# A hybrid decoder block in fp32 on one core: a buffer pool for the gates' results, gate 5 one product later, three buffers for pieces of the weights' sums

## The chip, the cores and the metric

The kernel runs on one core of a Trainium2 chip. A core has a matrix engine (TensorE, PE in the profile; its weight loads are PEld), three engines for elementwise work (VectorE or DVE, ScalarE or ACT, GpSimd or POOL) and a queue (SyncE, SP) that issues its transfers. Each engine works through its own instructions in a fixed order and waits for the others by semaphores. Matrix products land in PSUM, of which the kernel uses eight banks of 128 x 512 numbers; everything else on the chip is in SBUF, 128 partitions wide.

The metric is the time of one execution on the device, in microseconds. A run of the kernel gives one time; three runs were made of the kernel before.

## The reference

One layer of a block over 512 tokens of width 1024, in float32. Cut to what matters:

```python
h = rmsnorm(x, norm1_g)
z_glu, z_rx, z_rg, z_ga, z_gb = split(h @ w_in + b_in)    # 2048, 1280, 1280, 1024, 1024 wide

u = z_glu[..., :1024] * sigmoid(z_glu[..., 1024:])
u = causal_depthwise_conv(u, conv_dw_w, conv_dw_b)         # 31 taps
u = silu(layernorm(u, conv_ln_g, conv_ln_b))
y_a = u @ conv_w_out + conv_b_out

xb = causal_depthwise_conv(z_rx, lru_conv_w, lru_conv_b)   # 4 taps
r = sigmoid(blocks(xb, lru_wa) + lru_ba)                   # 16 blocks of 80 x 80
i = sigmoid(blocks(xb, lru_wx) + lru_bx)
log_a = -8 * r * softplus(-lru_lambda)
hb = scan(h_t = exp(log_a) * h_(t-1) + sqrt(-expm1(2 * log_a)) * i * xb)
y_b = (hb * gelu(z_rg)) @ lru_w_out

x = x + (sigmoid(z_ga) * y_a + sigmoid(z_gb) * y_b) @ w_mix_out
h = rmsnorm(x, norm2_g)
x = x + (silu(h @ ffn_w1) * (h @ ffn_w3)) @ ffn_w2         # 2816 wide
return rmsnorm(x, norm_f_g)
```

## The kernel before

**Products.** Tokens lie along the 512 columns, channels along the 128 partitions. To keep float32's precision every operand is kept as two parts, a high one (`h`, rounded to the fast matrix format) and a low one (`l`, the rest), and a product is three matrix instructions: high x high, high x low, low x high (`mm3`, L432). The high part is a cast on ACT (`split_to`, L115, cast at L117), the low part a subtraction (`sub`, L113) on DVE or POOL. A product of the input stage (1024 channels in, 128 out) is 24 instructions on PE.

**Weights** come in chunks. `emit_chunk` (L135) loads one into one of four raw buffers (SP's queue, L144), casts it on ACT and subtracts on POOL (input stage) or DVE (later), into one of five buffers `hl`. A product asks for its chunk, and so four chunks ahead are emitted with it (`AHEAD`, L35). A gate's chunk is a zeroed buffer into which 6 to 10 small loads (L188) put the blocks of 80 x 80; for even gates (counted within each half of five) a small copy on DVE (L193) follows.

**The input stage** (`ORDER`, L201 to 203, run at L763 to 782) lists its products by hand, and the chunks of weights are listed in the same order (L205 to 212):
- `u` j: two products of the conv branch and u_j (`glu`, L657; L664 on DVE). The 31-tap convolution over u is a generator, `beside` (L588), of which each entry of the list emits a few steps (L600 on DVE, in PSUM); after it come the layer norm's two column means, each a product with a matrix of ones (`column_mean`, L607; PSUM tiles lnmp and lnvp), and `un`, the operand of conv_w_out. The sums' split parts are the tiles lnms and lnvs.
- `rx` j: a product, the 4-tap convolution into `xb`j (L676 on ACT, L678 on DVE), its two parts xb`j`h and xb`j`l, and copies of some of their rows to other partitions (`ext_in`, L689; transfers at L701 into the tiles `ext`), since a block of 80 channels straddles tiles of 128.
- `g` j: the two gates r and i of channels tile j (`gates`, L706): eight or twelve instructions on PE into two banks, L726 to L731 on ACT, L732 to L735 on DVE. Their lasting results are two tiles, `th`j and `ea`j.
- `r` j: the recurrence (`recur`, L740): a square root on ACT into a bank `mu`j (L743), a product on DVE (L744) and the scan (L745).
- `rg`, `gb`, `ga` j: a product each; y_j (two parts) from `rg` (L756 to 760), the sigmoids sgb_j and sga_j from the others (L752).

Then come eight products with lru_w_out (`yb`, L785 to 794), eight with conv_w_out (`ya`, L896 to 904) and the mixing product (`mxr`).

**Sevenfold products.** w_mix_out, four of the feed-forward's tiles (`SEVEN`, L44) and ffn_w2 are multiplied with seven products of quarters in place of eight. That needs sums of the weights' quarters. For the feed-forward, `make_f_sums` (L315) makes them during the input stage: sixteen pieces, each two loads (L334) into a buffer of the pool `wsums`, four operations on POOL (L342 to 345) and a store (L349). One step of it is taken with each entry of `ORDER`. The pool has two buffers. The operands' sums are made in `Sevenfold.pair` (L825): the tiles us (two parts), s1p (two halves), e and va for each k; there are eleven k in the last product (names `ou`, `ov`, `ous`, `os1p`, `oe`). In `run` (L846) the tiles e and va are split in their turn (`oeb`, `ovb`), and with k = 0 the residual (x2b, eight tiles) and norm_f_g (gf, two) are loaded (`loads`, L1073).

**Buffers.** Most tiles of 128 x 512 that outlive a step come from one pool, `longt` (L95), with `SLOTS` = 65 buffers of 2 KB per partition; short-lived ones from `shortt`, with 5. Six PSUM banks belong to the pool `psum` (`bank`), two to `psum2` (`bank2`). The whole of SBUF is in use.

**The order of instructions.** Where the kernel says nothing else, a planner orders each engine's instructions when the kernel is compiled: it goes through a model of the run, takes on every engine the ready instruction that stands first in the program's text, and gives a new tile a buffer when one is free. The buffer, the order and the waits are then fixed. Parts of the kernel (norms, the ends of the sevenfold products) are ordered by hand (`manual_schedule`).

Of the kernel before, what the change touches and what calls it, by code (L numbers as in the profile page):

```python
# [28 lines left out]
NF = DF // P  # L29


SLOTS, SHORT = 65, 5
RAW = 4
HL = 5
AHEAD = 4  # L35
# [45 lines left out]
def tile_block(ctx, tc, a, out):  # L81
    nc = tc.nc
    pool = lambda name, bufs, **k: ctx.enter_context(tc.tile_pool(name=name, bufs=bufs, **k))
    consts = pool("consts", 1)
    raws = pool("raws", RAW)
    hls = pool("hls", HL)
    wsums = pool("wsums", 2)
    psum = pool("psum", 6, space=bass.MemoryType.PSUM)
    psum2 = pool("psum2", 2, space=bass.MemoryType.PSUM)

    def tiles(tag, bufs):
        p_ = pool(tag, bufs)
        return lambda name, dtype=F32: p_.tile([P, T], dtype, tag=tag, name=name)

    longt, shortt = tiles("long", SLOTS), tiles("short", SHORT)  # L95

    def pairt(name, dtype=F32R):

# [2 lines left out]
    def bank(name):  # L101
        return psum.tile([P, T], F32, tag="mm", name=name)
# [9 lines left out]
    def sub(eng, o, x, y):  # L112
        return eng.tensor_tensor(out=o, in0=x, in1=y, op=ALU.subtract)  # L113

    def split_to(h, l, full, eng, copy=act.copy):  # L115

        copy(h, full)  # L117
        last = sub(eng, l, full, h.bitcast(F32))
        if eng is pool_e:
            newest["sub"] = last.ins  # L120
        return h, l

    def split(name, full, eng, p_=None, copy=act.copy):
        p_ = p_ or pairt(name)
        return split_to(*p_, full, eng, copy)
# [35 lines left out]
    def weights(key, ahead=AHEAD):  # L161
        i = next(i for i, c in enumerate(chunks) if c[0] == key)
        emit_to(i + 1 + ahead)
        return held.pop(key)
# [14 lines left out]
    def gate_chunk(j):  # L179
# [18 lines left out]

    ORDER = """u0 u1 rx0 rx1 gb0 rx2 u2 g0 rx3 gb1 g1 u3 rx4 g2 gb2 r0 r1 u4 g3 rx5 rg0 g4 rx6 rg1 u5 r2 r3 g5 rx7  # L201
        gb3 rg2 rx8 g6 rg3 u6 r4 r5 g7 rx9 gb4 rg4 u7 g8 r6 r7 rg5 gb5 g9 rg6 gb6 r8 r9 rg7 gb7 ga0 rg8 ga1 rg9
        ga2 ga3 ga4 ga5 ga6 ga7""".split()
    ORDER = [(t.rstrip("0123456789"), int(t.lstrip("abcdefghijklmnopqrstuvwxyz"))) for t in ORDER]
    for kind, j in ORDER:  # L205
        if kind == "g":
# [336 lines left out]
    ab, e, s, s2, po, c4 = (sm[:, i, :] for i in range(6))  # L543
# [162 lines left out]
    def gates(j):  # L706
        hv, lv = (gate_view(v[:, 0, :]) for v in weights(f"gate{j}"))
        j5 = j % 5
        banks = []
        for g in range(2):  # L710
            ps = bank(f"g{j}_{g}")
            (wh, oh), (wl, ol) = ((v[:, g, 0, :], v[:, g, 1, :]) for v in (hv, lv))
            xh, xl = xbp[j]
            mms = [(wh, xh), (wh, xl), (wl, xh)]
            if j5 % 2:
                eh, el = ext[j]
                mms += [(l[:MANY], r[:MANY]) for l, r in ((oh, eh), (oh, el), (ol, eh))]
            else:
                mms.append((oh[: 3 * FEW], ext[j][0][: 3 * FEW]))
            for k, (l, r) in enumerate(mms):  # L720
                pe.matmul(ps, l, r, start=k == 0, stop=k == len(mms) - 1)  # L721
            banks.append(ps)

        r_, i_ = banks
        th = longt(f"th{j}")
        act.activation(th, r_, AF.Tanh, scale=0.5, bias=bh[:, 0, j : j + 1])  # L726
        act.activation(i_, i_, AF.Tanh, scale=0.5, bias=bh[:, 1, j : j + 1])  # L727

        A = longt(f"ea{j}")
        act.activation(A, th, AF.Exp, scale=c8[:, j : j + 1], bias=c8[:, j : j + 1])  # L730
        act.activation(r_, th, AF.Tanh, scale=c4[:, j : j + 1], bias=c4[:, j : j + 1])  # L731
        vec.scalar_tensor_tensor(out=r_, in0=A, scalar=1.0, in1=r_, op0=ALU.add, op1=ALU.mult)  # L732
        vec.scalar_tensor_tensor(out=xb[j], in0=i_, scalar=1.0, in1=xb[j], op0=ALU.add, op1=ALU.mult)
        vec.tensor_scalar(out=A, in0=r_, scalar1=1.0, scalar2=None, op0=ALU.add)
        vec.scalar_tensor_tensor(out=th, in0=A, scalar=1.0, in1=r_, op0=ALU.add, op1=ALU.mult)  # L735
        rec[j] = A, th

    rec = {}

    def recur(j):  # L740
        A, m2 = rec.pop(j)
        mu = bank(f"mu{j}")
        act.activation(mu, m2, AF.Sqrt, scale=-0.25)  # L743
        vec.tensor_tensor(out=mu, in0=xb[j], in1=mu, op=ALU.mult)  # L744
        vec.tensor_tensor_scan(xb[j], A, mu, 0.0, op0=ALU.mult, op1=ALU.add)  # L745
# [16 lines left out]
    f_sums_steps = make_f_sums()  # L762
    for kind, j in ORDER:  # L763
        next(f_sums_steps, None)
        if kind == "u":
            glu(j)
        elif kind == "rx":
            rx(j)
            run_beside(4)
        elif kind == "g":  # L770
            gates(j)
        elif kind == "r":
            recur(j)
        elif kind == "rg":
            rg(j)
            run_beside(6)
        elif kind == "gb":
            sig(GB, j, sgb, "sgb")
            run_beside(6)
        else:  # L780
            sig(GA, j, sga, "sga")
            run_beside(8)
# [27 lines left out]
    class Sevenfold:  # L810
# [14 lines left out]
        def pair(self, k, ua, va):  # L825

            n = self.name
            u_ = split(f"{n}us{k}", ua, vec)
            s1 = shortt(f"{n}s1{k}")[:, LO]
            add(s1, va[:, LO], va[:, HI])  # L830
            sp = longt(f"{n}s1p{k}", F32R)
            split_to(sp[:, LO], sp[:, HI], s1, vec)
            e = longt(f"{n}e{k}")
            sub(vec, e[:, HI], ua[:, LO], va[:, LO])
            sub(vec, va[:, LO], s1, ua[:, LO])
            sub(vec, e[:, LO], ua[:, HI], va[:, LO])
            self.ops.append((u_, sp, e, va))
# [58 lines left out]
    for n, j in enumerate(mixq.order()):  # L896
# [3 lines left out]
        o = sga[j]  # L900
# [262 lines left out]
```

## Time and profile before

| | us |
|---|---|
| three runs: lowest, median, highest | 814.56, 814.58, 815.5 |
| the profiled execution, on the device | 814.25 |
| its span, from the first to the last instruction | 812.5 |
| PE busy, DVE busy, ACT busy, POOL busy | 799.8, 647.2, 445.2, 210.4 |
| input stage's products on PE | 10 to 325 |
| products with lru_w_out, conv_w_out | 325 to 380, 380 to 423.5 |
| mixing product, feed-forward's first half | 423.5 to 463, 463 to 700.5 |
| product with ffn_w2 and the end | 700.5 to 812.5 |

The granted clock of TensorE was 0.998 of full speed. Times inside the execution are counted from its first instruction. In a list of waits a line reads: engine, tile and line that waited, what ended the wait, then microseconds in total, how often, the longest. In a timeline: start, duration, engine, line, operation, what it writes and reads, and in brackets how long the engine had been idle and what ended that. A chain of waits gives start, duration and what the time was spent in. Buffer numbers are left out of a tile's name where they stand at its end (xb for xb5), and kept inside it (xb7l).

### The profile page before, as it was taken

Reading aid. Unit: us, or ns where it says so; the run is one execution under the profiler, and the core shown is the slowest. Engines: PE = TensorE matmul, PEld = TensorE weight load, DVE = VectorE, ACT = ScalarE, POOL = GpSimd, SP = SyncE. Lnnn points to the kernel's source line nnn. Section 1 sums busy time; section 2 is a strip of 40 time slices with the busy share of each in tenths; the row PEclk is TensorE's granted clock in tenths of the full one; section 3 lists DMA queues with packets and bytes.
Section 4 is the critical chain, followed back from the end, with each engine's and each line's share of the span. In section 5 each row is a group of like instructions: output and inputs, shape, how many; then the busy total and the mean of one; then the engine's idle time right before and its main releaser. Section 6 shows DMA issues by size and latency. Waiting matters only on the chain.

```text
span 812.5 us, 11454 instructions
## 1 busy us (share of the span) xinstructions
PE 799.8 (98%) x4038; PEld 682.0 (84%) x4038; DVE 647.2 (80%) x1010; ACT 445.2 (55%) x627; POOL 210.4 (26%) x156
## 2 busy tenths in 40 slices
PE   8999999999999999999999999999999999999996
PEld 7988888887788888888888898999988888888885
DVE  4699899999999987786968769797866664688556
ACT  7546688777668755653326554464632233476443
POOL 3575778758666740000000042000000000000000
PEclk9999999999999999999999999999999999999999
DMA  7746566666655622358628425788778788576552
GB/s 214 190 128 164 143 176 199 172 189 193 185 169 156 183 74 65 111 177 275 215 93 259 156 88 181 237 266 247 226 235 279 250 274 284 195 255 211 169 168 104
DMA packets 182029, 153.46 MB, mean 189 GB/s; under 512 B 12519, under 2 KB 150163, under 8 KB 181971
## 3 DMA queue, kind: packets, MB, share of 16 engines
q1 hardware_dynamic: 181971, 152.72, 61.2%
q8 instruction: 32, 0.52, 0.3%
q14 instruction: 26, 0.21, 0.1%
HBM read 123.46 MB, written 26.21 MB: 184 GB/s over the span
## 4 chain that ended last, share of the span: by engine, by line
PE 93%; DVE 3%; issue 1%; ACT 1%; DMA 1%; SPq 0%; POOL 0%; POOLq 0%; ACTq 0%
PE z L441 32%; PE f L441 19%; PE or L844 13%; PE fr L1020 10%; PE yb L441 7%; PE ya L441 5%; PE mxr L844 5%; PE g L721 2%; DVE cv L600 1%; DMA raw_in<-in_w_in_dram 1%; PE th L481 0%; DVE xb8l L113 0%; PE tx L481 0%; DVE of L1086 0%; DVE x L497 0%
## 5 line engine op out<-in xcount | busy, mean ns | idle before, releaser
L600 DVE SCALAR_TENSOR_TENSOR cv<-u,par,cv 128x511 f32<-128x511 f32 (+17 forms) x240 | 162.5, 728 | 1.1 <-ACT cv L597 0.9
L113 POOL TENSOR_TENSOR hl_in<-raw_in,hl_in 128x1024 fp32r<-128x1024 f32 x52 | 125.5, 2416 | 91.1 <-ACT hl_in L117 90.5
L117 ACT CAST hl_in<-raw_in 128x1024 fp32r<-128x1024 f32 x52 | 54.2, 1042 | 9.4 <-PE z L441 6.6
L117 ACT CAST hl_f<-raw_f 128x1024 fp32r<-128x1024 f32 x28 | 29.3, 1051 | 49.8 <-DMA raw_f<-in_ffn_w_dram 31.3
L113 DVE TENSOR_TENSOR hl_f<-raw_f,hl_f 128x1024 fp32r<-128x1024 f32 x28 | 36.3, 1304 | 15.9 <-ACT hl_f L117 15.9
L994 POOL TENSOR_TENSOR hf<-h20h,h20l 128x512 f32<-128x512 f32 x1 | 1.3, 1288 | 172.4 <-DVE h20l L485 172.4
L117 ACT CAST hl_ob<-raw_ob 128x1024 fp32r<-128x1024 f32 (+1 forms) x23 | 23.4, 1016 | 39.0 <-PE or L844 18.7
L441 PE MATMUL z<-h10h,hl_in 128*128 128x512 f32 (+1 forms) x112 | 42.3, 379 | 1.7 <-DVE xb L745 1.2
L113 DVE TENSOR_TENSOR hl_ob<-raw_ob,hl_ob 128x1024 fp32r<-128x1024 f32 (+1 forms) x23 | 27.1, 1176 | 20.5 <-ACT hl_ob L117 20.4
L441 PE MATMUL z<-h11h,hl_in 128*128 128x512 f32 (+1 forms) x112 | 41.7, 374 | 0.0
L441 PE MATMUL z<-h15h,hl_in 128*128 128x512 f32 (+1 forms) x112 | 41.7, 374 | 0.0
L441 PE MATMUL z<-h17h,hl_in 128*128 128x512 f32 (+1 forms) x112 | 41.7, 374 | 0.0
L441 PE MATMUL z<-h14h,hl_in 128*128 128x512 f32 (+1 forms) x112 | 41.7, 374 | 0.0
L441 PE MATMUL z<-h16h,hl_in 128*128 128x512 f32 (+1 forms) x112 | 41.7, 374 | 0.0
L441 PE MATMUL z<-h12h,hl_in 128*128 128x512 f32 (+1 forms) x112 | 41.7, 374 | 0.0
L441 PE MATMUL z<-h13h,hl_in 128*128 128x512 f32 (+1 forms) x112 | 41.7, 374 | 0.0
L113 POOL TENSOR_TENSOR fws<-fws 128x256 f32<-128x256 f32 x48 | 36.3, 757 | 2.6 <-DMA fws<-in_ffn_w_dram 0.2
L113 DVE TENSOR_TENSOR ows<-ows,ows 128x512 f32<-128x512 f32 x22 | 15.2, 689 | 20.9 <-DMA ows<-in_ffn_w_dram 20.8
L113 DVE TENSOR_TENSOR hl_ot<-raw_ot,hl_ot 128x1024 fp32r<-128x1024 f32 (+1 forms) x17 | 20.1, 1190 | 11.8 <-ACT hl_ot L117 11.4
L117 ACT CAST hl_ot<-raw_ot 128x1024 fp32r<-128x1024 f32 (+1 forms) x17 | 17.5, 1028 | 17.2 <-PE or L844 13.9
L441 PEld LDWEIGHTS z<-h10h,hl_in 128*128 128x128 f32 x112 | 21.1, 188 | 6.5 <-ACT g L727 1.6
L441 PEld LDWEIGHTS z<-h11h,hl_in 128*128 128x128 f32 x112 | 21.1, 188 | 3.8
(905 smaller groups left out, 2577.4 us busy)
## 6 DMA issues: line engine op xcount, KB each, us to landing
raw_in<-in_w_in_dram SPq DMA_DIRECT2D x52, 512.0 KB
raw_f<-in_ffn_w_dram SPq DMA_DIRECT2D x28, 512.0 KB
ows<-in_ffn_w_dram SPq DMA_DIRECT2D x22, 512.0 KB
ot<-ows SPq DMA_DIRECT2D x44, 256.0 KB
raw_ob<-in_ffn_w_dram SPq DMA_DIRECT2D x33, 256.0 KB
raw_ot<-ot SPq DMA_DIRECT2D x33, 256.0 KB
fws<-in_ffn_w_dram SPq DMA_DIRECT2D x32, 256.0 KB
fs<-fws SPq DMA_DIRECT2D x16, 512.0 KB
```

The costliest lines, as they stand in the source:

```text
L113: return eng.tensor_tensor(out=o, in0=x, in1=y, op=ALU.subtract)
L117: copy(h, full)
L441: pe.matmul(ps, l, r, start=i == 0, stop=i == n - 1)
L600: vec.scalar_tensor_tensor(out=acc[c][:, s:], in0=u[c][:, : T - s], scalar=dw(c, s), in1=acc[c][:, s:], op0=ALU.mult, op1=ALU.add)
L721: pe.matmul(ps, l, r, start=k == 0, stop=k == len(mms) - 1)
L844: pe.matmul(banks[i], l_[:, ts], r_, start=start and n == 0, stop=stop and n == 2, skip_group_check=again)
L994: pool_e.tensor_tensor(out=v, in0=h2p[c][0].bitcast(F32), in1=h2p[c][1].bitcast(F32), op=ALU.add)
L1020: pe.matmul(ps[:, HALVES[i]], lw[:, 4 * i + c, :], rx_, start=not (again or i or c or m), stop=bool(i and c == 3 and m == 2), skip_group_c ...
```

## The change

- `th`j and `ea`j of the ten gates come from a pool of their own, `gatet`, with six buffers. In the last sevenfold product, the tiles e of k = 0 to 5 use the same six buffers. The long pool goes from 65 to 57 buffers.
- In `ORDER`, `g5` moves behind `rx7`; with it, gate 5's chunk of weights comes behind rx7's.
- The pool `wsums` goes from two buffers (4 KB each) to three.

The buffers' sum stays the same: 65 x 2 KB + 2 x 4 KB before, (57 + 6) x 2 KB + 3 x 4 KB after.

```diff
-SLOTS, SHORT = 65, 5
+
+SLOTS, SHORT, GATES = 57, 5, 6
...
-    wsums = pool("wsums", 2)
+    wsums = pool("wsums", 3)
...
-    longt, shortt = tiles("long", SLOTS), tiles("short", SHORT)
+    longt, shortt, gatet = tiles("long", SLOTS), tiles("short", SHORT), tiles("gate", GATES)
...
-    ORDER = """u0 u1 rx0 rx1 gb0 rx2 u2 g0 rx3 gb1 g1 u3 rx4 g2 gb2 r0 r1 u4 g3 rx5 rg0 g4 rx6 rg1 u5 r2 r3 g5 rx7
+    ORDER = """u0 u1 rx0 rx1 gb0 rx2 u2 g0 rx3 gb1 g1 u3 rx4 g2 gb2 r0 r1 u4 g3 rx5 rg0 g4 rx6 rg1 u5 r2 r3 rx7 g5
         gb3 rg2 rx8 g6 rg3 u6 r4 r5 g7 rx9 gb4 rg4 u7 g8 r6 r7 rg5 gb5 g9 rg6 gb6 r8 r9 rg7 gb7 ga0 rg8 ga1 rg9
         ga2 ga3 ga4 ga5 ga6 ga7""".split()
...
-        th = longt(f"th{j}")
+        th = gatet(f"th{j}")
...
-        A = longt(f"ea{j}")
+        A = gatet(f"ea{j}")
...
-            e = longt(f"{n}e{k}")
+            e = (gatet if n == "o" and k < GATES else longt)(f"{n}e{k}")
```

## The prediction

> **What bounds the kernel now.** I read the page first, then TensorE's (PE's) waits, then the chain of waits, then the timelines of the stretches that these point at, and last how long each tile lives.
>
> ```profile
> span 812.5 us, 11454 instructions
> PE 799.8 (98%) x4038; PEld 682.0 (84%) x4038; DVE 647.2 (80%) x1010; ACT 445.2 (55%) x627; POOL 210.4 (26%) x156
> PE   8999999999999999999999999999999999999996
> DVE  4699899999999987786968769797866664688556
> ```
>
> PE has work for 799.8 of 812.5 us, at full clock. An edit that moves no product between the first slice and the last can give back only PE's waits in between. VectorE (DVE) is full from slice 3 to 13 (40 to 285 us).
>
> PE's waits between 30 and 460 us, then those of tile ext6l, then what PE's chain came through before 205 us:
>
> ```profile
> PE z L441 <- DVE xb L745: 1.2, 1, 1.2
> PE g L721 <- DVE th L735: 0.3, 1, 0.3
> ```
>
> ```profile
>   DMA ext6l<-xb7l: 0.5, 1
> ```
>
> ```profile
> 184.80 1.31 POOL hl_gate L113
> 190.28 2.69 DVE xb8l L113
> ...
> 203.07 1.20 DVE mu L744 x2
> 204.28 1.14 DVE xb L745
> 205.41 0.14 issue
> ```
>
> So gate 6 waits at 183 for a copy into ext6l (against the pace of 0.227 us per product it loses 0.37), and gate 7 and rx9 wait at 202.4 to 205.5 for PSUM banks (0.49 + 0.11 + 1.39 + 0.08 = 2.07). 0.37 + 2.07 = 2.44 us is everything that the input stage can return.
>
> ScalarE's (ACT's) timeline shows why DVE is late with gate 6:
>
> ```profile
> 185.56 0.66 ACT L727 ACTIVATE g<-g,bh 128x512 f32<-128x512 f32 x1 [1.28 <-PE g L721]
> 186.14 1.04 ACT L117 CAST hl_in<-raw_in 128x1024 fp32r<-128x1024 f32 x1
> 189.06 0.62 ACT L117 CAST xb8h<-xb 128x512 fp32r<-128x512 f32 x1 [1.88 <-DVE xb L678]
> ...
> 191.63 0.68 ACT L726 ACTIVATE th<-g,bh 128x512 f32<-128x512 f32 x1
> ```
>
> The text has th6 (L726) before L727; the trace has it 6 us after. In the text, th6 is taken from the long pool behind xb8's halves. The same shows elsewhere: th1 (90.53) comes right behind sgb1 (89.94), th9 (254.81) behind sgb5 (253.28), though their products ended at 85.58 and 247.55. I read this as: tiles of one pool are handed out in the order of the text, so a gate's tanh waits for whatever long tile stands before it.
>
> **The change part by part.** Sums are made against the profiled execution: 814.25 us, of which 812.5 span and 1.75 around it. It lies 0.33 below the median of the runs, 814.58.
>
> *Gates' own pool.* No instruction is added. th6 can run at about 184.3, when ACT is through with xb8's L676, instead of 191.63. DVE's L732, L734 and L735 of gate 6 (200.05, 201.24, 202.48, some 0.6 us each) then come before gate r4's scan has its input, and not between. r4's L744 and scan stand behind 3 x 0.6 = 1.8 us less, and the scan ends at 205.40 - 1.8 = 203.6. The bank that rx9's product waits for is the one that this scan releases (z14's bank lay free from 202.83, so which bank it gets was fixed beforehand). The product starts at 203.65 and not 205.55: 1.9 us gained, all earlier waits included. Bounds: 0 (conv steps fill the freed time, the scan stays at 205.40, and the earlier waits only move into this one) and 2.44 (no wait left). A loss is not excluded: a conv pair more ahead of the scan costs 1.3. I take 1.9, what the rows themselves give. Do six gate tiles suffice? In the trace at most three gates live at once (g4, g8), and ea7 (206.34) finds ea4 released at 205.40. This holds by 0.9 us there, and by more elsewhere.
>
> *Gate 5 behind rx7.* PE's work is the same. rx7's 24 products move ahead by gate 5's 8 (1.85 us), its chunk ahead of gate 5's on SP, ACT and POOL, and so do xb7, its split and its copies into ext6. SP issues ext6l at 178.83 and PE reads it at 183.38, 0.37 late. 1.85 us covers that. Gate 5 itself goes from 158.6 to 164.0. What it feeds is r5, whose sqrt runs at 200.24. th2 and ea2 (released 152.5 and 159.74) are out by then. The gain is counted in the 1.9; alone it would be 0.37.
>
> *Three buffers for pieces.* In SP's waits:
>
> ```profile
> SPq L334 <- DMA fs<-fws: 30.2, 10, 5.6
> ```
>
> Ten loads of pieces wait for a buffer to be stored, and everything behind them in SP's queue waits too: at 172.21 six of gate 7's small loads, rx9's weights and ext6's copies (177.56 to 179.38). A third buffer lets each load go one piece sooner. PE waits for no weight load between 30 and 460 us, so this is worth 0 beyond the 0.37 already counted; if the cover went, a load is 5.6 us late at most, against splits that are ready at least 4.7 us before their product (hl_lo5_0).
>
> *The price: long slots, 65 to 57.* I counted the tiles alive in the trace without gates' tiles and without oe0 to oe5.
> (1) At 302.94 us: y 20, h1 16, u 8, sgb 8, sga0 to 3, lnmt: 57. The next is lnmsh, at 307.36. No slot comes free before the last input product lets go of h1:
>
> ```profile
> 307.36 0.62 ACT L117 CAST lnmsh<-lnmt 128x512 fp32r<-128x512 f32 x1 [3.73 <-DVE lnmt L623]
> ```
>
> ```profile
> 319.77 0.39 PE L441 MATMUL z<-h10l,hl_in 128*128 128x512 f32 x1
> ```
>
> So the layer norm's mean (lnmp, 313.62) waits for 320.16 + 0.62 + 0.69 = 321.5, 8 us later, and sga4 to 7 with it. That keeps four banks, and yb0 and yb1 take the other two, so PE goes on. Behind lnmsh on ACT stand the casts of hl_lo0_0 and hl_lo0_1 (307.89, 309.10) and sga4; if they had to wait along, the splits would be done by 323 and 324, for products at 325.0 and 328.4. Behind it, DVE idles 4.36 us before 315 now, and 5.75 us between 320 and 336, which take in the work that moves. The tightest cover is hl_lo5_0: split done at 354.8, product at 359.5. By idle time DVE gets there (0.8 before lnmp + 1.5 at lnvp) 2.3 us later; 4.7 us cover it. Cost 0. PE's queue gets two products where their input is just ready (lnmp, lnvp); the trace's like is the 0.3 us at 475 us where a product follows its h20h. 0 to 0.6, I take 0.15. Further bound: all 8 us arrive at hl_lo5_0, 8 - 4.7 = 3.3 lost.
> (2) At 670.39: h2 16, 4 x 6, 5 x 3, ou9 and ov9: 57. ous9's split waits from 682.0 to h20's release at 695.48. DVE then has 0.69 + 0.35 + 3 x 0.42 = 2.3 us more before f3_10's bank comes free (697.62, so 699.9); the last bank of the next stage is wanted at 703.71. Behind ous9h on ACT stand the next stage's casts: hl_ob11_0 is ready 10.3 us before its product, the wait is 13.5 us. Cost 0, bound 3.2 if the casts wait along.
> (3) The out stage: the splits of late e and v tiles are done at 737 now. With eight slots less, four new tiles find three released by each product step (4.08 us) plus the v tile just split, and run a step or so behind, to about 745. They are read from 745 (first) to 786 (last). Cost 0.
>
> [...]
>
> Sum: -1.9 + 0.15 = -1.75. 814.25 - 1.75 = 812.5 profiled, and 812.5 + 0.33 = **812.8** as a median.
>
> **The rivals.**
> *The bank wait stays* (0.22). DVE is full, and its work up to r4's scan is the same; conv steps take the place that L732 to L735 leave. Then the product still starts at 205.55 and nothing comes back: 814.6. For it: 14 of DVE's instructions between 186 and 205 are conv steps. Against: r4's sqrt was done at 200.31 and DVE came at 203.00.
> *The layer norm comes through* (0.10): 3.3 us lost at yb5, 812.8 + 3.3 = 816.1; half of it, 814.5.
> *The two-input rule* (0.08). xb8l's split took 2.79 us and xb7l's 2.22 where xb2l's took 0.68; both ran while POOL subtracted (190.02 to 192.43, 173.31 to 175.72). Pieces and chunks move on POOL, so other splits can be hit: 2.1 us each on DVE's way to r4's scan. From the second new hit on PE loses: 812.8 + 4.2 - 1.9 = 815.1, and a third ends slower, 817.2. Against: the two worst hits of ten are there already. [...]
> *Slower: the out stage runs out of slots* (0.16). Splits of e and v cost DVE 1.2 us for each k. If they pile up behind 737, they meet the sums there: DVE has 2.55 us idle between 737 and 745, and hl_ot2_0 is ready 2.93 us before its product. All ten: 12 - 5.5 = 6.5 us, 812.8 + 6.5 = 819.3. It is slower by 0.2% once 3.4 + 5.5 = 8.9 us, some eight of ten, pile up. For it: x2b's and gf's ten tiles stand ahead of them. Against: releases come every 4 us, as counted.
>
> **How the numbers follow.** No change, for this kernel, is within 0.2% or 1.63 us (812.95 to 816.21). Forecast 0.44 (811.9 to 813.3, mostly below 812.95), and the rivals as above. Faster: 0.39 of the forecast and 0.05 of the two middle rivals that end better than priced: 0.44. Slower: 0.16, with 0.04 of the layer norm and 0.03 of the rule: 0.23. Same: 0.33. Low end 811.9: 814.25 - 2.44 + 0.33 = 812.1 and 0.2 for scatter. High end 817.2, the rule's third hit; above it lies most of the out stage's 0.16. The forecast's own range is 811.9 to 813.3.
>
> **What would show it.** Right: th6 within 1 us of g6_0's end; no DMA wait for ext6l; z25's wait under 0.5 us; L334's waits far under 30 us; lnmsh after the first of ga7's products, lnmp some 8 us later against its neighbours, no PE wait from 320 to 425; ous9's split after h20's release. Wrong: PE waits near 205 of more than 1 us, near 336 or 360, at 745, or new ones between 60 and 300, where DVE's order changes in more places than I priced.

## The result, and the profile after

Before 814.36 us (median of six runs, 813.67 to 815.5), after 820.25 us (six runs, 818.07 to 821.12). The ratio is 1.0066 with a 95% interval of 1.0055 to 1.0077: the change makes the kernel slower, by 4.5 to 6.3 us, where 812.8 had been forecast. Line numbers after are those of before plus one.

The head of the changed kernel's page (span, busy times, and the busy tenths of PE and DVE in 40 slices):

```profile
span 818.8 us, 11457 instructions
PE 802.5 (98%) x4038; PEld 683.8 (84%) x4038; DVE 647.6 (79%) x1010; ACT 442.2 (54%) x625; POOL 210.9 (26%) x156
PE   8999999999899999999999999999999999999996
DVE  5699799999979984895888869787866664679556
```

PE does the same 4038 instructions in a span 6.3 us longer. Its waits (engine, tile, line, what ended the wait; total, times, longest):

```profile
PE z L442 <- DVE xb L746: 4.5, 2, 3.3
PE fr L1021 <- ACT c L1033: 0.9, 1, 0.9
```

The wait for a scan's bank (L745 before, 1.2 us once) is now there twice, and a new one stands in the feed-forward. The first of the two was not there at all before.

To see where the 6.3 us arise I compared when the same product starts in both traces, from the first instruction on. The table gives each place's share:

| place (us in the changed kernel) | what PE does there | us against before |
|---|---|---|
| 0 to 30 | start; differs from run to run | -0.43 |
| 165.5 | product of gb3 waits for the bank of r3's scan | +1.77 |
| 183 | gate 6 finds ext6l there in time | -0.44 |
| 204.2 to 211.3 | rx9's product waits for the bank of r4's scan, then runs at half pace | +2.99 |
| 318 to 330 | lnmp's two products stand among ga7's, their input just ready | +0.33 |
| 461 | a late product of the mixing stage; its cause is open | +0.29 |
| 545 | second use of a feed-forward bank waits for ScalarE's copy | +1.19 |
| 813 to the end | last stores | +0.59 |

They sum to 6.3. The dearest place, in PE's timeline (start, duration, what, idle time before):

```profile
204.23 0.39 PE L722 MATMUL g<-ext,hl_gate 96*128 96x512 f32 x1
207.94 0.77 PE L442 MATMUL z<-h10h,hl_in 128*128 128x512 f32 x1 [3.31 <-DVE xb L746]
208.50 0.63 PE L442 MATMUL z<-h10l,hl_in 128*128 128x512 f32 x1
208.93 0.63 PE L442 MATMUL z<-h10h,hl_in 128*128 128x512 f32 x1
```

and in the view by stretches (PE, PEld, DVE, ACT, POOL busy with counts, then the granted clock, DMA share, GB/s):

```profile
204.20:207.80 3.60, 0.42 (x2) 0.00 (x0) 3.60 (x6) 3.57 (x6) 3.28 (x3) 0.99 0.26 72
207.80:211.20 3.40, 3.26 (x8) 2.62 (x9) 3.40 (x5) 3.37 (x5) 3.24 (x4) 0.51 0.28 69
```

The wait itself is 3.48 us beyond PE's pace. Then the products follow each other by 0.427 us, not 0.227, until 211.06, because the granted clock is 0.51. This second part is 0.34 + 6 x 0.2 + 0.04, some 1.6 us. The wait brings its own surcharge.

Why are the scans late? DVE is busy all the while, so look at its order. Before, between 123 and 136 us, the work that others wait for was interleaved with the conv steps (L600):

```profile
123.66 0.75 DVE L664 SCALAR_TENSOR_TENSOR u<-z,par,sg 128x512 f32<-128x512 f32 x1
124.33 3.31 DVE L600 SCALAR_TENSOR_TENSOR cv<-u,par,cv 128x501 f32<-128x501 f32 x5
132.52 0.74 DVE L678 SCALAR_TENSOR_TENSOR xb<-z,par,xb 128x511 f32<-128x511 f32 x1
```

After, fifteen conv steps stand ahead of u4 with nothing but a small cast between them, and rx5's xb comes 5.8 us later:

```profile
120.52 3.96 DVE L601 SCALAR_TENSOR_TENSOR cv<-u,par,cv 128x504 f32<-128x504 f32 x6
124.84 5.88 DVE L601 SCALAR_TENSOR_TENSOR cv<-u,par,cv 128x501 f32<-128x501 f32 x9
130.75 0.75 DVE L665 SCALAR_TENSOR_TENSOR u<-z,par,sg 128x512 f32<-128x512 f32 x1
138.29 0.75 DVE L679 SCALAR_TENSOR_TENSOR xb<-z,par,xb 128x511 f32<-128x511 f32 x1
```

Counted from the start of the kernel, eight more conv steps stand ahead of u4 than before, and six more (4.4 us) ahead of rx5's xb; no other operation has come ahead of either.

ScalarE's cast of xb5 waits for that, and everything behind it in ScalarE's queue with it. Before (first line, no wait shown) and after:

```profile
135.94 0.62 ACT L117 CAST xb5h<-xb 128x512 fp32r<-128x512 f32 x1
```

```profile
141.72 0.62 ACT L118 CAST xb5h<-xb 128x512 fp32r<-128x512 f32 x1 [6.33 <-DVE xb L679]
```

So the theory was: with the pool of their own, the gates' tanh no longer waits for its place in the text; the planner, which orders the instructions at compile time, then fills DVE's queue otherwise and puts conv steps ahead of what is urgent on the chip. The rivals: the exchange of gate 5, the third buffer, or the eight long slots do it.

### The profile page after: what moved, and what is told of

Same layout as the page of the kernel before. It is cut to its first block, busy times and chain, and to the rows that moved or that the text cites. A ratio compares the mean times of both kernels' runs of the same rounds, so it can differ in the third digit from the quotient of the medians.

```text
span 818.8 us, 11457 instructions
## 1 busy us (share of the span) xinstructions
PE 802.5 (98%) x4038; PEld 683.8 (84%) x4038; DVE 647.6 (79%) x1010; ACT 442.2 (54%) x625; POOL 210.9 (26%) x156
## 4 chain that ended last, share of the span: by engine, by line
PE 83%; DVE 5%; DMA 4%; POOL 2%; ACT 2%; SPq 2%; issue 2%; POOLq 0%; ACTq 0%
PE z L442 25%; PE f L442 19%; PE or L845 13%; PE fr L1021 7%; PE yb L442 7%; PE ya L442 5%; PE mxr L845 5%; PE g L722 2%; DMA raw_in<-in_w_in_dram 1%; DVE cv L601 1%; POOL hl_in L114 1%; DMA fs<-fws 1%; SPq L398 1%; DMA fws<-in_ffn_w_dram 1%; DMA raw_fb<-in_ffn_w_dram 1%
## 5 line engine op out<-in xcount | busy, mean ns | idle before, releaser
L118 ACT CAST hl_lo<-raw_lo 128x640 fp32r<-128x640 f32 x16 | 11.6, 728 | 28.2 <-PE z L442 9.4
```

## Experiments: the parts alone

Each kernel is timed against the kernel before on the same chip; the ratios are to that. "Wait" of PE means the time beyond its pace.

**The exchange alone.** `ORDER` as changed, SLOTS 65, no pool for gates, two buffers for pieces.

> Only the exchange of gate 5 and the product behind it in the input's order; 65 long slots, no pool of the gates' own, two buffers for the pieces of the weights' sums. The theory (the pool of the gates' own is what costs: it changes the order of VectorE's work, so that scans and banks come later): 0.4 us less than before, since the wait of 0.37 us for ext6l at 182.9 us goes and nothing else moves; the waits at 163.6 (1.76 us in the changed kernel) and 544 (1.21 us) aren't there, the one near 204 stays at 2.0 to 2.5 us. The rival (the exchange costs, since gate 5's work now lies a product later on VectorE and pushes the scans of r4 and r5): 2 us or more above before, with the wait near 204 at 4 us or more.

812.43 us against 814.49; ratio 0.9977 (0.9966 to 0.9989): faster, and by some five times the 0.4 us expected. The wait for ext6l is gone, and the one near 204 falls from 2.08 to 0.55 us. PE's wait for a scan's bank in this kernel:

```profile
PE z L442 <- DVE xb L746: 0.3, 1, 0.3
```

Gate 6's th6 comes no earlier here (192.17 against 191.63), yet r4's scan runs at 202.28 and not at 204.19. Between gate 7's cast near 186 us and that scan DVE does eleven conv steps and not thirteen, and gate 6's first operation (L732 before) comes at 197.40 in place of 199.96. So the gain of the prediction's first step exists, but it belongs to the exchange.

**The gates' pool alone.** SLOTS 59, GATES 6, two buffers for pieces, `ORDER` as before.

> Only the pool of the gates' own, six buffers, also for the first six oe tiles; 59 long slots, two buffers for pieces, the input's order as before. The theory (this part alone carries the loss, through VectorE's order): 4 to 6.5 us above before, with waits of TensorE for a scan's bank near 164 (1.4 to 2 us) and near 204 (3 us or more, then products at half pace for some 3 us), and the 0.39 us at 182.9 still there. The rival (the loss needs the exchange or the third buffer): within 1 us of before, and the wait near 204 gone or at most 2.1 us.

819.02 us; ratio 1.0051 (1.0039 to 1.0063). The size is as the theory expected, the places are not: there is one wait, before gate 5, of 4.27 us beyond the pace, followed by some seven products at half pace, and one of 0.98 at 543.

```profile
PE g L722 <- POOL fws L114: 4.1, 1, 4.1
PE fr L1021 <- ACT c L1033: 0.7, 1, 0.7
```

The tile that this gate waits for is ext: its copies from xb6 are issued at 159.4 to 162.8. xb5h is cast at 141.74, after a wait of 6.31 us, just as in the changed kernel. The same lateness of DVE, met by a gate that stands one product earlier. It comes there through SyncE's queue: xb5's last copy goes out at 144.19 (138.39 before), and the copies from xb6, which stand behind it, begin at 159.40 (153.29 before). It holds PE up so long that the later scans aren't waited for.

**The third buffer alone.** `wsums` 3, SLOTS 63.

> Only the third buffer for the pieces of the weights' sums, paid for with two long slots (63); the rest as before. The theory: within 0.3 us of before, as was predicted for this part; SyncE's wait for the second piece's load (30.2 us in before) falls under 10 us, TensorE's waits stay as before. The rival (the loads that come earlier push the loads of the feed-forward's weights or VectorE's order): 1 us or more above before, with the wait of 1.2 us near 544 for ScalarE's copy, which would then be this part's.

815.23 us; ratio 1.0013 (1.0004 to 1.0021), a small loss. PE's waits are as before (4.39 us in all against 4.38), and SyncE's wait for these loads falls from 30.2 us to 11.5, not under 10. So neither expectation is met: nothing is pushed, and still some 0.6 us are lost, all of it behind PE's last product. The last stores are looked at below.

**Pool and exchange.** SLOTS 59, GATES 6, two buffers for pieces.

> The pool of the gates' own and the exchange, with two buffers for pieces and 59 long slots. The theory (the pool costs, the exchange saves 0.4, the third buffer nothing): 0.3 to 0.5 us below the pool alone, and within 0.5 us of the changed kernel (6 us above before). The rival (the third buffer brings the wait near 544 and its 1.2 us): 1.2 us or more below the changed kernel, and no wait near 544.

818.66 us; ratio 1.0052 (1.0037 to 1.0066), not to be told from the pool alone. The waits are at 166 (1.75), 205.5 (4.24, with half pace) and 544 (1.25), as in the changed kernel, and 0.66 for ext6 at 185. So the third buffer brings none of them, and the exchange's gain can't be seen beside the pool's loss. The median is 1.6 us under the changed kernel's, where 0.5 at most had been expected; 0.6 of that are the end (below), and 0.6 are PE's delays at 318 to 330 and 461, which this kernel does not have.

**Six long slots fewer, and nothing else.** SLOTS 59.

> Only six long slots fewer (59), nothing else of the change; the memory that comes free isn't used. The theory: within 0.4 us of before; no wait near 544, since that comes from the order in which the gates' work stands. The rival (the wait of 0.98 us near 543 in the run of the pool alone comes from the fewer long slots): 0.7 us or more above before with that wait in the trace.

814.91 us; ratio 1.0007 (0.9997 to 1.0016): no difference that can be told, no wait near 544. The number of long slots isn't the cause.

**Exchange and third buffer.** SLOTS 63.

> The exchange and the third buffer for pieces, with 63 long slots and no pool of the gates' own. The theory (the parts add up as long as VectorE's order stays): 2.1 - 0.7 = 1.4 us under before, between 0.8 and 2 us. The rival (the exchange's gain hangs on where the loads lie, and the third buffer takes it): within 0.5 us of before.

813.29 us; ratio 0.9984 (0.9975 to 0.9993), 1.35 us less. These two parts add up. The pool does not add to either.

## Experiments: the order put back

**The pool with the old order.** In the program with six long slots fewer every engine keeps its order up to 313 us. So it was not room that the common pool decided in the input stage, but which writer comes first. That can be put back without the common pool: ScalarE's first writers of the tiles concerned issue in the order of the text.

```diff
+    def in_turn(key, make):
+        if key not in latest:
+            last = make()
+        else:
+            with tc.issue_after(latest[key]):
+                last = make()
+        latest[key] = last.ins
+        return last
...
-        act.activation(th, r_, AF.Tanh, scale=0.5, bias=bh[:, 0, j : j + 1])
+        in_turn("act", lambda: act.activation(th, r_, AF.Tanh, scale=0.5, bias=bh[:, 0, j : j + 1]))
...
```

and likewise for ea, xb, xbh, yh and the sigmoids. The same was written for VectorE's u, xbl and yl; it moves no instruction of the program, so what counts is ScalarE's order. In the changed kernel this moves 26 of ScalarE's instructions, and some 90 of VectorE's follow.

> The pool of the gates' own as in the run of the pool alone (six buffers, 59 long slots), but the order that the common pool had enforced is put back by hand: ScalarE's first writers of xb, xbh, yh, sgb, th and ea may issue only in the order of the text, and so may VectorE's first writers of u, xbl and yl. All is computed as before. The theory (what costs is that tanh and exp of a gate, and VectorE's four operations behind them, are no longer held back to their place in the text, so that VectorE does them and then conv steps ahead of rx's and the scans' work): within 1 us of before, at least 3 us under the pool alone, and no wait of TensorE of more than 0.6 us between 140 and 200 us. The rival (the pool costs by itself, by its fewer long slots or where its buffers lie): 3.5 to 5 us above before, with the waits near 159 and 543 still there.

813.62 us; ratio 0.9987 (0.9978 to 0.9996): the 4.2 us are gone and 1.1 more. One wait is a little over the bound given: gate 5's for ext, 0.69 us (0.61 + 0.08) at 159.2. The wait near 204 is 0.30. xb5h is cast at 137.82, after 1.85 us of waiting. PE's waits for ext:

```profile
PE g L736 <- DMA ext<-xb6h: 0.4, 1, 0.4
```

**The whole change with the old order.**

> The whole change, with the same order put back by hand on ScalarE and VectorE. All is computed as before. The theory, with the parts measured alone (exchange 2.1 us less, third buffer 0.7 us more, the pool's cost gone with the order): 1 to 2 us under before, 6 us or more under the changed kernel; waits of TensorE near 164 and 204 under 0.6 us each, that of 0.3 us near 324 (the mean's product with 57 long slots) stays. The rival (the three parts cost in other ways than by this order): 3 us or more above before.

813.45 us; ratio 0.9985 (0.9976 to 0.9994), 6.8 us under the changed kernel's 820.25. Of PE's waits only these are left beyond 0.3 us: 0.31 at lnmp, and the 1.51 near 480 that the kernel before has too. Near 164 and 204 there is nothing. The rival, that the parts cost in other ways, falls.

The two orders also say what stood in the scans' way. Ahead of r3's scan VectorE does five conv steps (3.6 us) more in the changed kernel than here, and nothing else more or less; ahead of r4's, three conv steps (2.2 us) more and one product (0.7 us) less. No operation of a gate is among them. r3's scan runs at 165.75 in the changed kernel and at 161.43 here, and r4's, in the changed kernel and here (the second line holds r4's and r5's):

```profile
206.58 1.22 DVE L746 TENSOR_TENSOR_SCAN xb<-ea,mu 128x512 f32<-128x512 f32 x1
203.75 2.32 DVE L760 TENSOR_TENSOR_SCAN xb<-ea,mu 128x512 f32<-128x512 f32 x2
```

In both compiled programs gb3's and rx9's products take the banks that these two scans release.

**Pool and exchange with the old order.**

> The pool of the gates' own and the exchange, with the order on ScalarE put back by hand (what is held on VectorE beside it leaves the program as it is) and two buffers for pieces, 59 long slots. The theory (with the order put back, the pool's cost is gone and the exchange's gain stays): 1.8 to 2.8 us under before, as the exchange alone (2.1 us) or up to 0.7 us better, since the scan's bank near 204 comes earlier with the pool. The rival (pool and exchange gain the same 2 us twice over, or hinder each other): within 1.2 us of before.

812.93 us; ratio 0.9983 (0.9974 to 0.9992), 1.55 us less where 1.8 to 2.8 were expected. PE's waits near 160 and 204 are all gone, yet it is no better than the exchange alone (812.43): with the order kept, pool and exchange remove the same wait, and it can be removed only once.

**The conv steps held back.** The order of ScalarE as in the changed kernel; beside it each conv step stays behind the last scan, split of xb or product u that stands before it in the text (`newest["urgent"]`, set at these three places).

```diff
-                    vec.scalar_tensor_tensor(out=acc[c][:, s:], in0=u[c][:, : T - s], scalar=dw(c, s), in1=acc[c][:, s:], op0=ALU.mult, op1=ALU.add)
+                    with tc.issue_after(newest["urgent"]):
+                        vec.scalar_tensor_tensor(out=acc[c][:, s:], in0=u[c][:, : T - s], scalar=dw(c, s), in1=acc[c][:, s:], op0=ALU.mult, op1=ALU.add)
```

> The whole change; beside it VectorE's conv steps (the three shifted multiply-adds of each channel of the conv branch) may not issue ahead of the scans, the splits of xb and the products of u that stand before them in the text. All is computed as before. The theory in its second half (the harm is done by conv steps that stand in VectorE's queue ahead of the scans and of xb5's and xb6's splits): the waits near 164 and 204 fall from 6.8 us together to under 1.5 us, and the time to 813 to 816 us, unless the conv steps that now come late push the layer norm behind them. The rival (it is the gates' own four operations, not the conv steps, that stand in the way): both waits stay at 5 us or more together, and the time at 818 us or more.

816.01 us; ratio 1.0019 (1.001 to 1.0028), at the upper end of what the theory gave. Both waits for a scan's bank are gone, from 6.8 us to nothing. But the run does not show that the scans come earlier, for they come later: r3's at 170.19 (165.75 in the changed kernel), r4's at 213.81 (206.58). The conv steps held back at first pile up ahead of the scans:

```profile
201.59 6.58 DVE L604 SCALAR_TENSOR_TENSOR cv<-u,par,cv 128x506 f32<-128x506 f32 x10
213.81 2.32 DVE L750 TENSOR_TENSOR_SCAN xb<-ea,mu 128x512 f32<-128x512 f32 x2
```

What comes earlier is u4 (127.42 for 130.75) and the splits of xb5 and xb6 (137.56 and 151.97 for 143.41 and 157.10). The two products no longer wait because the planner, with the order changed, gave them other banks: one of u5's two products' (free at 164.15) and one of u6's (free at 204.58). So a late scan costs only where a product has been given its bank, and that is fixed by the same plan. The rival's signs did not come, but that conv steps make the scans late rests on the comparison under the whole change with the old order, not on this run. The price is a wait at another place, gate 6's for ext6h (1.85 us), and the one at 541 (1.58) remains:

```profile
PE fr L1025 <- ACT c L1037: 1.3, 1, 1.3
PE g L726 <- DMA ext6h<-xb7h: 1.2, 1, 1.2
```

## Experiments: the wait near 544, and the end

In all kernels with the gates' pool, also those with the old order, one copy of ScalarE's had changed places in the feed-forward. Before, the copy c (L1032), which empties a bank that the next product writes, came ahead of os1p's cast:

```profile
536.84 0.57 ACT L1032 COPY c<-fr 128x512 f32<-128x512 f32 x1
537.98 0.41 ACT L117 CAST os1p<-os 128x256 fp32r<-128x256 f32 x1 [0.57 <-DVE os L800]
```

After, the cast waits for DVE and the copy stands behind it:

```profile
544.32 0.41 ACT L118 CAST os1p<-os 128x256 fp32r<-128x256 f32 x1 [1.10 <-DVE os L801]
544.63 0.58 ACT L1033 COPY c<-fr 128x512 f32<-128x512 f32 x1
```

**The oe tiles left in the long slots.** As pool and exchange, with one line taken back:

```diff
-            e = (gatet if n == "o" and k < GATES else longt)(f"{n}e{k}")
+            e = longt(f"{n}e{k}")
```

> The pool of the gates' own and the exchange, two buffers for pieces, 59 long slots, but the oe tiles of the feed-forward's output stay in the long slots. All is computed as before. The theory (with oe in the gates' pool, ScalarE's copy of os1p, which waits for VectorE, comes to stand ahead of the copy c that TensorE's second product waits for; it does in all seven kernels with that pool, which wait 0.2 to 1.6 us near 540, and in none of the six others, which wait 0): the wait near 544 goes, the waits near 164 and 204 (1.75 and 4.24 us in the run of pool and exchange) stay; 0.9 to 1.5 us under that run, 2.6 to 3.5 us above before. The rival (the copy comes late because the first stage is late): the wait near 544 stays at 0.9 us or more.

817.94 us; ratio 1.0047 (1.0032 to 1.0061). The wait near 544 is gone; those at 166 and 205.5 stay (1.68 and 2.76). The median is 0.7 us under that of pool and exchange, less than the 0.9 to 1.5 expected and within what the two intervals leave open. The profiled executions show the share of this place clearly: from 500 to 540 us pool and exchange lose 1.23 us against before, this kernel 0.00. The rival, that the first stage's lateness does it, falls. It is a second case of the same kind: where a tile's buffer comes from decides where its writer is placed in the queue.

**The same with the old order in the first stage.**

> The same with the order on ScalarE in the first stage put back by hand. All is computed as before. The theory (both orders mended, the exchange's gain and the pool's earlier scan kept): no wait of TensorE between 140 and 320 us over 0.3 us and none near 540; 2.0 to 3.0 us under before, 0.25 us better than with oe in the gates' pool. The rival: within 1 us of before, or a new wait in the output stage, where oe then waits for long slots.

812.67 us; ratio 0.9978 (0.9968 to 0.9988), 1.7 us under before where 2.0 to 3.0 were expected. No wait between 140 and 320 us, none near 540. This and the exchange alone have the lowest medians, and they can't be told apart, nor from pool and exchange with the old order; all three beat the kernel before and the changed one. The exchange alone is one moved word.

**The last stores.** Every kernel with the third buffer so far ends 0.5 to 0.6 us later behind PE's last product than the others. The four last stores on SyncE's queue, before and with the third buffer alone:

```profile
807.32 1.81 SPq L1102 DMA_DIRECT2D out_dram<-of  x4
```

```profile
807.67 2.05 SPq L1103 DMA_DIRECT2D out_dram<-of  x4
```

The issue takes 0.24 us more, and the last store lands later by the rest. A gap of some 0.3 us lies between the stores: behind the first store in one kernel, ahead of the last in another (in the changed kernel 0.41 us pass behind the first store, where the kernel before has 0.10). Its place moves by as many records as the kernel's SyncE has more or fewer of them.

> The exchange and the third buffer for pieces (63 long slots); the two loads of the last norm's weights, late in the kernel and far from its end, are cut into eight parts each, which gives SyncE 14 instructions more. All is computed as before. All four kernels with the third buffer (862, 859, 864 and 863 records of SyncE) have a gap of about 0.3 us between SyncE's last stores, at a place that moves with their number of records, and end 0.53 to 0.64 us later after TensorE's last product than the five others (867 to 874 records, no gap). The theory (the gap lies at a fixed place of SyncE's program and is met early with more instructions, where SyncE waits anyway): the gap and the 0.6 us at the end go, 0.3 to 0.8 us less than without these parts, near the exchange alone. The rival (the third buffer makes the last stores late by itself): gap and 0.6 us stay.

```diff
-            nc.sync.dma_start(gf[h], a["norm_f_g"][h * T : (h + 1) * T].partition_broadcast(P))
+            for r in range(0, P, P // 8):
+                nc.sync.dma_start(gf[h][r : r + P // 8], a["norm_f_g"][h * T : (h + 1) * T].partition_broadcast(P // 8))
```

The gap between the stores and the 0.6 us at the end are gone, as the theory had it: from PE's last product on, this kernel and the one before agree to 0.00 us. The time is worse all the same, 819.11 us, ratio 1.0062 (1.0049 to 1.0075), since the loads hold SyncE's queue to 716.7 us and the next chunks' loads come behind them: the casts of hl_ob run at 727.24, and PE loses 6.4 us from 724 on, half pace included. So the run shows the place of the gap, and its edit is no remedy. What SyncE does in the gap no view of the profile shows; that stays open.

## Why the prediction was wrong

*Gates' own pool, -1.9 us (bounds 0 to -2.44).* This is the step that failed. Alone the pool costs 4.2 us. The reading behind it, that a gate's tanh is held to its place in the text, is right in the main: putting just that order back removes the loss, and in the changed kernel th1 and th2 start 0.04 and 0.9 us behind their products (4.95 and 9.6 before). It is wrong for th9, given as a sign of it: th9 starts 7.26 us behind its product in both kernels, behind a cast (y5h) that waits 3.4 us for VectorE. And the step it was made for did not come: th6 starts at 190.59 in the changed kernel, 5.5 us behind its product, not at 184.3, since a cast ahead of it in ScalarE's queue (y2h) waits 2.38 us for VectorE.

The conclusion was wrong in what follows from the reading. I moved one gate's work (th6) in the trace and left all other rows where they were; but th and ea of every gate come free of their place, the order is made at compile time, and some 130 of DVE's 1010 instructions move in the program with the pool alone (44 in that with six long slots fewer, all behind 313 us). Some 90 still stand elsewhere when ScalarE's old order is put back, without a loss: not the number that move costs, but the conv steps that come to stand ahead of what others wait for. The prediction even named the cost ("a conv pair more ahead of the scan costs 1.3") and then left it out of the bounds. Even in the kernel with the pool and the old order th6 runs at 189.79, not at 184.3, so the sum's first number fell too.

*Gate 5 behind rx7, 0.37.* The sign and the place are right, ext6l isn't waited for any more. The size is not: alone it gives 2.1 us, because r4's scan comes earlier with it. The 1.9 that I had put down to the pool is this step's.

*Three buffers for pieces, 0.* SyncE's waits for these loads did fall, from 30.2 us (10 times) to 8.5 (5 times) over the whole run; in the stretch from 30 to 215 us from 17.8 us (7 times) to

```profile
SPq L335 <- DMA fs<-fws: 4.1, 4, 2.2
```

and PE gained nothing from it, as said. The 0.6 us at the end weren't foreseen.

*Long slots, +0.15.* Right in its cost in all three places. lnmsh waits for h1's release and is cast at 323.8; lnmp and lnmsl cost PE 0.29 us there, inside the 0 to 0.6 given. ous9 is split at 701.7, where before's time for h20's release (695.48) and the shift of 5.7 us by then make 701.2. The splits of the out stage run later than said: the last starts at 754.90, with the shift taken off 749.2, where about 745 had been said. It is read from 791.7 on, and PE waits for none. Where oe0 to oe5 lie was costed with the slots, at nothing; that they stand in the gates' pool costs 1.2 us, by ScalarE's order.

*The rivals.* "The bank wait stays" had the right mechanism, conv steps that take the place of what moves, and the wrong bound: it let the scan stay where it was, while it ended 1.5 us later against PE (2.4 us later, with PE 0.9 behind), and the wait grew with the clock's surcharge from 2.07 to 5.05 us. The layer norm's delay did not come through: PE keeps its distance to before from 340 to 461 us. What the prediction called the two-input rule brought nothing either, and no run shows such a rule; the 2.1 us for each hit are the difference of two rows (2.79 and 0.68). What the traces show is that the ten splits of xb took 13.4 us in the changed kernel and 13.6 before; xb6l's went from 1.33 to 2.67 us, xb8l's from 2.79 to 0.68. The slower rival, an out stage without slots, did not happen. What would show it wrong was named: waits of more than 1 us near 205, and new ones between 60 and 300 where DVE's order changes. Both came.

## What to carry to other kernels

A pool that many tiles share does two things: it gives room, and it lets their writers come only in the order of the text. Taking tiles out of it changes an order that no line of the kernel states, so price it as a new order of every engine in that stage, with a loss inside the range, and not as one instruction moved in the old trace. When such a change is worth having for its room, put the order back by hand (here holds on ScalarE's first writers, 6.8 us), and do the parts one at a time: one moved word held all of the gain.

## What the runs showed of the hardware

**When a wait halves TensorE's clock.** Pool and exchange, with and without oe, wait at the same place by nearly the same time: 3.01 us from the start of one product to that of the next, and 2.91. Behind the first, seven products run at half the clock, which costs some 1.4 us; behind the second none do. The length alone doesn't decide that. In the traces' records the granted clock changes only at steps of 3.413 us: in the changed kernel it is full from 13.158 to 207.718 us, which is 57 such steps, then half for one, then full for 604.159 us, 177 steps; with the pool alone it is full for 157.013 us, 46 steps, and then half for one; before it is full from 7.238 to 809.370 us, 235 steps. Where no change is recorded, the borders are an estimate, counted on by steps of this length. Cut at these steps, the two kernels read (stretch, PE busy, PEld, DVE, ACT, POOL, then the granted clock; first with oe, then without):

```profile
204.60:208.00 3.40, 1.26 (x6) 0.70 (x4) 3.40 (x6) 3.37 (x5) 3.02 (x2) 1.00 0.35 100
208.01:211.42 3.41, 2.94 (x7) 2.39 (x8) 3.41 (x6) 3.38 (x5) 3.17 (x5) 0.50 0.57 155
```

```profile
203.51:206.92 3.41, 2.44 (x11) 1.69 (x9) 3.41 (x6) 3.38 (x5) 2.55 (x3) 1.00 0.70 217
206.92:210.33 3.41, 1.86 (x8) 1.58 (x9) 3.41 (x5) 3.39 (x5) 3.17 (x5) 1.00 0.61 165
```

With oe the wait lies in one step, of which PE is busy for 1.26 us, and the next step is slow. Without oe the wait lies across a border, 2.44 and 1.86 us stay busy, and the clock stays full. PE's idle time up to the border is 2.15 us with oe (3.41 - 1.26); without oe it is 0.97 us ahead of the border and 1.55 behind it, 2.52 together. In the three other kernels with a slow step between 30 and 800 us, PE was busy for 0.32 us (the changed kernel), 0.67 (the pool alone) and 0.73 (more loads) of the step ahead of it; there the waits were 3.7, 4.5 and 4.2 us from start to start. A step in the run with more loads in which it was busy for 1.84 us had no slow one behind it, and waits of 1.6 us left the clock alone. So, by an estimate from these runs alone, the limit between 30 and 800 us lies between 1.26 and 1.84 us of busy time in a step of 3.41. It does not fit the start of the changed kernel: there PE is busy for 1.85 us of the step from 6.33 us, and the next step is slow (clock 0.50). What sets the clock no trace here shows.

**The gap in SyncE's last stores** (0.3 us, at a place that moved with the number of its instructions) is told above, its cause open.
